# Two layers in one kernel: 64-row products of the state space stage and of the dilated attention, taken in turns between the halves of the array

## The chip, the core and the metric

One core of a Trainium2 chip runs the whole kernel. Its engines are named as in the profile: PE multiplies matrices (PEld is its weight load), DVE and ACT are the two elementwise engines, POOL a third one that does almost nothing here, and SP issues the DMAs. The metric is device time in microseconds (us), the median of several executions. A smaller number is better.

## The reference, cut to what matters

`reference()` is one layer after another on 256 tokens of width 1024, batch 1, all in float32.

```python
x = first_block(...)    # causal attention, gated linear attention, memory attention, a feed-forward of 4096
x = second_block(x, ...)
# second_block:
h = rms_norm_2(x, norm_w)
u_s, z_s, q, k, v, z_a, r_s, r_a = split(h @ w_in)
y_s = s5_branch(u_s, ...)            # per group of 16 channels: h_t = A h_(t-1) + B u_t (64 complex states), Re(C h) + D u
y_s = (y_s * silu(z_s)) @ w_ssm_out
y_a = dilated_attention(rope(norm(q)), rope(norm(k)), v)   # three groups of heads: every, every 4th, every 16th position
y_a = (y_a * silu(z_a)) @ w_attn_out
x = x + (sigmoid(r_s) * y_s + sigmoid(r_a) * y_a) @ w_o
```

The change touches `s5_branch` (64 groups of 16 channels, 64 complex states each) and `dilated_attention` (three groups of 8 heads of 64).

## The kernel before, in words

The layers are written one after the other by the class `Net`, as a list of operations without an order. A planner (`Plan`) then works backward from the end to give each operation a latest time (`latest`), and forward to put them into one order per engine (`order`). It goes by prices in ns that `price` (from L264) gives each instruction, by lags between engines, and by how many buffers there are of each kind (`BUFS`: 8 PSUM banks, 26 large and 11 small SBUF buffers). An engine then runs its instructions strictly in that order, and waits where an operand is late. So a price that changes moves instructions in all engines. Operations written as `nc.any` go to DVE or ACT, as the planner finds. Every instruction is recorded by one helper, hence the line L535 in all rows.

Most of PE's time goes to products with weights (`gemm_feat`, `gemm_tok`). They are split into a high and a low part (tiles `wh`, `wl`) by ACT and DVE, and use the whole array of 128 x 128.

Four functions of the second layer matter here.

- `ssm_quarter` (once for each of four quarters of the groups, `qd`) prepares tables. It has 16 products of 64 rows by 32 columns with 128 moving columns (`p[32 * j:32 * j + 32]`, `kn`). `gh` (0 or 1) picks partitions 0 to 63 or 64 to 127.
- `ssm_scan` (once for each quarter) has 32 products of 64 rows, 64 columns and 64 moving columns into `xp` (`G` with the input `U`); then a chain of DVE work (complex products and two prefix scans, TENSOR_TENSOR_SCAN in the profile) that makes the states `H`; then 48 products of the same size into `y`: for each `gh` and each of eight `g` one of `U` with the table `T`, and two of `H` with `Cx` that are added to it. For `gh` = 0 both operands and the result lie in partitions 0 to 63: the product uses the quarter of the array with rows and columns 0 to 63, called block (0, 0) below. For `gh` = 1 it is block (64, 64). `U` comes back from a bounce through DRAM (`ud`), `T` from another (`kz`).
- `dilated` (four pairs of heads `b`) makes, for each head `i` of a pair and each half `tt` of the tokens, a score tile `p`: one product of all 128 rows, 256 wide (`k2T[0]`), and four of 64 rows, 64 columns, 64 wide. These four have one row half (by the head `i`) and take turns between two column halves (by `c`).
- `block2` starts the parts in turns (`ORDER2`); the planner decides what really stands where.

A float32 product stands in the trace as two matmuls, called halves below: 384 products of 64 x 64 x 64 are 768 rows of the trace. 320 of them belong to `ssm_scan` and 64 to `dilated`.

Of the kernel before, what the change touches and what calls it, by code (L numbers as in the profile page):

```python
# [19 lines left out]
P = 128  # L20
S = 256
# [154 lines left out]
class Plan:  # L176
# [105 lines left out]
    @staticmethod  # L282
    def price(op):

        size = lambda v: int(np.prod(v.shape[1:]))
        if op.name == "dma_start":
            return {SP: 50, ACT: 50, POOL: 1000}[op.eng]
        if op.name == "matmul":
            out, l, r = op.args
            n, cols, half = size(r), size(l), l.shape[0] <= 64  # L290
            if r.buf.dtype == F32R:
                return 13 + n / 2.4
            if cols == 32:
                return 27 if n == 32 else 60
            if cols <= 64 and n <= 64:
                return 110 if half else 142

            if half:
                return 2 * (2 * n / 2.4 + cols / 1.2 - 8)
            return 2 * (max(2 * n / 2.4, cols / 1.2) + 9)  # L300
        if op.name == "transpose":
            return 110
        n = max(size(v) for v in op.outs + op.ins)
        psum = any(v.buf.tag == "ps" for v in op.outs + op.ins)
        if op.eng == ACT:
            c = (51 if psum else 93) + 0.833 * n
            c += 93 * (isinstance(op.kw.get("scale"), View) or isinstance(op.kw.get("bias"), View))
            return c + 93 * ("accum_out" in op.kw)
        if op.eng == POOL:
            return 10 + 0.9 * n if op.name == "memset" else 130 + 2.13 * n  # L310
        ptr = 63 * any(isinstance(a, View) and size(a) == 1 for a in op.args[2:])
        if op.name in ("tensor_copy", "tensor_scalar") and not psum:
            return 68 + 0.52 * n + ptr
        if op.name == "reciprocal":
            return 68 + 6.3 * n
        if op.name == "memset":
            return 10 + 1.05 * n
        return 68 + 1.042 * n + ptr
# [237 lines left out]
class Net:  # L556
# [810 lines left out]
    def ssm_quarter(self, qd):  # L1367
        nc, I = self.nc, self.I
        mag4, pw, f, ph = self.ssm_p
        gs = slice(8 * qd, 8 * qd + 8)  # L1370
        bt, ct = self.bT[:, :, gs], self.cT[:, :, gs]
        over = lambda v, sh: v.unsqueeze(len(v.shape)).to_broadcast(sh)
        sh = [P, 8, 16]
        mk = lambda: self.t2(sh)

        bb = self.t2([P, 2, 8, 16])
        self.cmul((bb[:, 0], bb[:, 1]), (bt[:, 0], bt[:, 1]), (over(f[0][:, gs], sh), over(f[1][:, gs], sh)), mk)
        bbt = self.t2([P, 2, 4, 16, 2])
        for ri in range(2):
            nc.any.copy(bbt[:, ri].rearrange("p j q a -> p j a q"), bb[:, ri].rearrange("p (j a) q -> p j a q", a=2))  # L1380

        cx = self.t4([P, 8, 2, 4, 16])
        nc.any.copy(cx[:, :, 0, 0], ct[:, 0])
        nc.any.copy(cx[:, :, 1, 0], ct[:, 1], -1.0)
        sh3 = [P, 8, 3, 16]
        c0 = tuple(cx[:, :, i, 0:1].to_broadcast(sh3) for i in range(2))
        p3 = tuple(over(pw[:, 1:4, i, gs].rearrange("p t g -> p g t"), sh3) for i in range(2))
        self.cmul((cx[:, :, 0, 1:], cx[:, :, 1, 1:]), c0, p3, lambda: self.t2(sh3), conj=True)

        g0 = self.t4([P, 2, 8, 4, 16])  # L1390
        sh4 = [P, 8, 4, 16]
        b4 = tuple(bb[:, i].unsqueeze(2).to_broadcast(sh4) for i in range(2))
        p4 = tuple(over(pw[:, 5:9, i, gs].rearrange("p t g -> p g t"), sh4) for i in range(2))
        self.cmul((g0[:, 0], g0[:, 1]), b4, p4, lambda: self.t2(sh4))
        gx, g = self.t4([P, 8, 2, 64]), self.t4([P, 8, 2, 64])
        for ri in range(2):
            p = self.mmp([P, 4, P])
            for j in range(4):
                nc.tensor.transpose(p[:, j], g0[:, ri, 2 * j:2 * j + 2].rearrange("p g s q -> p (g s q)"), self.ident)
            nc.any.copy(gx[:, 4 * ri:4 * ri + 4].rearrange("p j g n -> p j (g n)"), p)  # L1400
        for gh in range(2):
            for par in range(2):
                nc.sync.dma_start(out=g[64 * gh:64 * gh + 64, :, par], in_=gx[64 * par:64 * par + 64, :, gh])

        kn = self.t2([P, 2, P])
        for gh in range(2):
            p = self.mmp([P, P])
            hs = slice(64 * gh, 64 * gh + 64)
            for ri in range(2):
                for j in range(4):  # L1410
                    nc.tensor.matmul(p[32 * j:32 * j + 32], bbt[hs, ri, j].rearrange("p q a -> p (q a)"),
                                     cx[hs, 2 * j:2 * j + 2, ri].rearrange("p a t c -> p a (t c)"),
                                     start=ri == 0, stop=ri == 1, skip_group_check=True)
            nc.any.copy(kn[:, gh], p)
            v = kn[:, gh].rearrange("p (a x) -> p a x", a=2)[:, :, 0:16]
            nc.vector.scalar_tensor_tensor(v, self.diag, self.g("d_skip", 4 * gh + qd), v, ALU.mult, ALU.add)
        for par in range(2):
            nc.sync.dma_start(
                out=self.kz[:, par, 4 * qd:4 * qd + 4, :, 48:112].rearrange("g j q x -> (j q) g x"),
                in_=kn[par::2, :, 64 * par:64 * par + 64])  # L1420

        r = self.t4([P, 2, 8, 64])
        nc.vector.memset(r[:, 0, :, 0:1], 1.0)
        nc.vector.memset(r[:, 1, :, 0:1], 0.0)
        k = 1
        for i in range(6):
            shk = [P, 8, k]
            z = tuple(over(ph[:, i, ri, gs], shk) for ri in range(2))
            self.cmul((r[:, 0, :, k:2 * k], r[:, 1, :, k:2 * k]), (r[:, 0, :, 0:k], r[:, 1, :, 0:k]), z, lambda: self.t2(shk))
            k *= 2  # L1430
        self.G.append(g)
        self.Cx.append(cx)
        self.R.append(r)
# [44 lines left out]
    def ssm_scan(self, qd):  # L1478
        nc = self.nc
        mag4 = self.ssm_p[0]  # L1480
        U, G, Cx, R = self.U[qd], self.G[qd], self.Cx[qd], self.R[qd]
        X = self.t4([P, 2, 8, 64])
        xp = [self.aux([P, 8, 64]) for _ in range(2)]
        for ri in range(2):
            for gh in range(2):
                hs = slice(64 * gh, 64 * gh + 64)
                for g in range(8):
                    nc.tensor.matmul(xp[ri][hs, g], G[hs, 4 * ri + g // 2, g % 2], U[hs, g], start=True, stop=True)
            nc.any.copy(X[:, ri], xp[ri])
        mk = lambda: self.t2([P, 8, 64])  # L1490
# [9 lines left out]
        H = self.t4([P, 2, 8, 64])  # L1500
# [1 line left out]
        v = lambda a: a[:, :, 0:63]  # L1502
        self.cmul((H[:, 0, :, 1:], H[:, 1, :, 1:]), (v(st[0]), v(st[1])), (v(R[:, 0]), v(R[:, 1])), lambda: self.t2([P, 8, 63]))
        y = self.aux([P, 8, 64])
        for gh in range(2):
            hs = slice(64 * gh, 64 * gh + 64)
            for g in range(8):
                o = y[hs, g]
                nc.tensor.matmul(o, U[hs, g], self.T[g % 2][hs, 4 * qd + g // 2], start=True, stop=False, skip_group_check=True)
                for ri in range(2):  # L1510
                    nc.tensor.matmul(o, H[hs, ri, g], Cx[hs, g, ri].rearrange("p t c -> p (t c)"), start=False, stop=ri == 1, skip_group_check=True)
        ys = self.t2([P, 4, 8, 16])
        nc.any.copy(ys, y.rearrange("p g (t c) -> p t g c", t=4))
        p = self.aux([P, 4, 2, 64])
# [62 lines left out]
    def dilated(self):  # L1577
# [5 lines left out]
        half = [slice(0, 64), slice(64, P)]  # L1583
        for b in range(4):
            pts = []
            for i, a in enumerate(half):
                prs = []
                for tt in range(2):
                    p = self.aux([P, 384])
                    nc.tensor.matmul(p[:, 0:S], self.q2[0][:, b, tt * P:tt * P + P], self.k2T[0][i][:, b],  # L1590
                                     start=True, stop=False, skip_group_check=True)
                    for j in range(2):
                        for c in range(2):
                            g = 1 + (j ^ c)
                            cs = slice(tt * P + 64 * c, tt * P + 64 * c + 64)
                            nc.tensor.matmul(p[half[c], S + 64 * j:S + 64 * j + 64], self.q2[g][a, b, cs], self.k2T[g][a, b, cs],
                                             start=False, stop=j == 1, skip_group_check=True)
                    pr = self.t2([P, 384])
                    self.softmax_rows(p, pr, [384], self.dmask[:, tt])
                    prs.append(pr)  # L1600
                p0, p1 = self.aux([P, 2, S]), self.aux([P, 2, P])
                for tt in range(2):
                    for kb in range(2):
# [219 lines left out]
```

## Time and profile before

| | |
|---|---|
| median of three runs | 880.23 us (878.02 to 880.57) |
| the profiled execution | 878.85 us, its span 877.1 us |
| PE / DVE / ACT busy | 98% / 73% / 54% of the span |
| granted clock of PE, mean | 0.994 |

The span runs from the first to the last instruction; 1.75 us of the profiled execution lie around it. The first layer ends and the second begins at about 490 us. `ssm_scan` lies between 535 and 646 us, `dilated` between 690 and 725 us, and from there to the end only products with weights are left on PE. Ends of matmuls are modelled, so the pace of PE is best read from the distances of starts.

### The profile page before, as it was taken

The page shows a single profiled execution, that of the slowest core. Times are in us where ns is not written, and L with a number is a line of the kernel's source. Part 1 is how long each engine was busy: PE and PEld are TensorE (multiplying, and loading weights), DVE is VectorE, ACT ScalarE, POOL GpSimd, SP SyncE. Part 2 cuts the span into 40 slices and gives each one's busy share as a digit, 9 for nine tenths or more (in the row PEclk, how much of TensorE's full clock was granted, in tenths as well). Part 3 has the DMA queues.
Part 4 walks back from the last instruction along what each step waited for, and adds up shares of the span by engine and source line. Part 5 has one row for each costly group of instructions (what it writes and reads, how often), then busy time and mean ns, then how long its engine had stood idle before and what let it go on. Part 6 is the DMA issues. An engine that isn't in the chain of part 4 may idle for free.

```text
span 877.1 us, 16677 instructions
## 1 busy us (share of the span) xinstructions
PE 861.0 (98%) x6572; PEld 774.6 (88%) x6572; DVE 636.2 (73%) x1487; ACT 471.6 (54%) x751; POOL 5.4 (1%) x13
## 2 busy tenths in 40 slices
PE   8999998999999999999999998999999999999998
PEld 6988877889999889999999897888889769999996
DVE  6999999994766679954445745898995675653584
ACT  6767756644355466555555542453474663554352
POOL 2000000000000000000000000000000000000000
PEclk9999999999999999999999998999999999999999
DMA  9774432045355565665655579633436503665551
GB/s 322 249 233 145 156 134 98 1 146 191 122 176 184 192 196 192 188 199 189 190 192 191 184 160 248 191 98 114 130 105 190 161 25 105 185 193 183 175 178 64
DMA packets 60750, 144.19 MB, mean 164 GB/s; under 512 B 24560, under 2 KB 25712, under 8 KB 60672
## 3 DMA queue, kind: packets, MB, share of 16 engines
q1 hardware_dynamic: 60672, 143.13, 52.1%
q8 instruction: 51, 0.84, 0.4%
q14 instruction: 27, 0.22, 0.1%
HBM read 138.46 MB, written 2.56 MB: 161 GB/s over the span
## 4 chain that ended last, share of the span: by engine, by line
PE 80%; DVE 12%; DMA 3%; issue 2%; ACT 2%; SPq 1%; DVEq 0%; ACTq 0%
PE ps L535 80%; DVE k L535 7%; DVE wl L535 3%; DVE sm L535 2%; DMA wr<-w_k 1%; ACT k L535 1%; SPq L535 1%; DMA wr<-w_mv 1%; DMA k<-kz 1%; DVE c L535 1%; ACT wh L535 1%; DVEq L1811 0%; ACT c L535 0%; DVEq L535 0%; ACTq L535 0%
## 5 line engine op out<-in xcount | busy, mean ns | idle before, releaser
L535 DVE TENSOR_TENSOR wl<-wr,wh 128x1024 fp32r<-128x1024 f32 (+2 forms) x257 | 301.1, 1195 | 165.6 <-ACT wh L535 163.2
L535 ACT CAST wh<-wr 128x1024 fp32r<-128x1024 f32 (+2 forms) x257 | 257.5, 1028 | 222.6 <-PE ps L535 202.8
L535 PE MATMUL ps<-k,wh 128*128 128x256 f32 x2048 | 371.2, 283 | 0.0
L535 PEld LDWEIGHTS ps<-k,wh 128*128 128x128 f32 x2048 | 320.4, 192 | 1.8 <-ACT c L535 0.3
L535 PE MATMUL ps<-wh,k 128*128 128x512 f32 (+2 forms) x1024 | 314.1, 385 | 2.1 <-ACT wh L535 2.1
L535 PE MATMUL ps<-k,wl 128*128 128x256 f32 x1024 | 290.1, 283 | 0.0
L535 PEld LDWEIGHTS ps<-wh,k 128*128 128x128 f32 x1024 | 190.0, 189 | 38.5 <-ACT wh L535 3.0
L535 PE MATMUL ps<-wl,k 128*128 128x512 f32 (+2 forms) x512 | 197.0, 386 | 1.3 <-DVE wl L535 1.3
L535 PEld LDWEIGHTS ps<-k,wl 128*128 128x128 f32 x1024 | 196.4, 192 | 0.8 <-issue 0.3
L535 PEld LDWEIGHTS ps<-wl,k 128*128 128x128 f32 x512 | 96.6, 189 | 21.1 <-DVE wl L535 3.9
L535 PE MATMUL ps<-k,k 64*64 64x64 f32 (+6 forms) x1224 | 100.4, 256 | 4.4 <-issue 2.3
L535 DVE TENSOR_TENSOR k<-k,k 128x512 f32<-128x512 f32 (+8 forms) x192 | 91.3, 498 | 18.0 <-ACT k L535 17.5
L535 PEld LDWEIGHTS ps<-k,k 64*64 64x64 f32 (+4 forms) x1224 | 78.6, 141 | 21.6 <-issue 12.1
L535 ACT ACTIVATE k<-ps 128x512 f32<-128x512 f32 (+2 forms) x86 | 44.6, 532 | 48.2 <-PE ps L535 48.0
L535 ACT COPY k<-ps 128x512 f32<-128x512 f32 (+7 forms) x97 | 44.2, 497 | 43.9 <-PE ps L535 43.5
L535 ACT ACTIVATE k<-k 128x512 f32<-128x512 f32 (+3 forms) x70 | 46.2, 676 | 32.6 <-DVE k L535 31.8
L535 PE MATMUL ps<-c,k 128*128 128x128 f32 (+1 forms) x344 | 53.4, 285 | 3.5 <-DVE k L535 3.3
L535 PEld LDWEIGHTS ps<-c,k 128*128 128x128 f32 x344 | 41.1, 147 | 11.3 <-DVE k L535 4.8
L535 DVE TENSOR_TENSOR k<-k,c 128x64 f32<-128x64 f32 (+7 forms) x176 | 47.8, 316 | 0.4 <-ACT k L535 0.4
L535 ACT ACTIVATE k<-ps,c 128x256 f32<-128x256 f32 (+3 forms) x78 | 37.8, 544 | 13.6 <-PE ps L535 11.5
L535 DVE SCALAR_TENSOR_TENSOR k<-k,k 128x256 fp32r<-128x256 f32 (+4 forms) x61 | 33.3, 568 | 13.6 <-ACT k L535 13.2
L535 ACT ACTIVATE k<-k,sm 128x384 f32<-128x384 f32 (+2 forms) x32 | 17.0, 531 | 12.7 <-DVE sm L535 12.6
(74 smaller groups left out, 306.2 us busy)
## 6 DMA issues: line engine op xcount, KB each, us to landing
wr<-w_up SPq DMA_DIRECT2D x32, 512.0 KB, 4.0
wr<-w_down SPq DMA_DIRECT2D x32, 512.0 KB, 4.1
wr<-w_gt SPq DMA_DIRECT2D x24, 512.0 KB, 3.8
wr<-w_o SPq DMA_DIRECT2D x16, 512.0 KB, 4.0
wr<-w_k SPq DMA_DIRECT2D x12, 512.0 KB, 4.3
wr<-w_q SPq DMA_DIRECT2D x12, 512.0 KB, 4.4
wr<-w_v SPq DMA_DIRECT2D x12, 512.0 KB, 3.6
wr<-w_qkg SPq DMA_DIRECT2D x8, 512.0 KB, 4.6
```

The source lines that it names most:

```text
L535: getattr(getattr(tc.nc, op.eng), op.name)(*map(live, op.args), **{k: live(v) for k, v in op.kw.items()})
```

## The change

`price` gets 57 in place of 110 ns for a 64-row product with 64 columns, and 30 in place of 60 for those of `ssm_quarter`. In `ssm_quarter` and `ssm_scan` the loop over `gh` becomes the innermost one, so that consecutive products use opposite halves of the rows. In `dilated` the score tiles of both heads of a pair are written together, and the loop over the head is innermost; the softmax follows for both. Neither the products nor their sizes change.

```diff
-                return 27 if n == 32 else 60
+                return 27 if n == 32 else 30
             if cols <= 64 and n <= 64:
-                return 110 if half else 142
+                return 57 if half else 142
...
         for ri in range(2):
-            for gh in range(2):
-                hs = slice(64 * gh, 64 * gh + 64)
-                for g in range(8):
+            for g in range(8):
+                for hs in halves:
                     nc.tensor.matmul(xp[ri][hs, g], G[hs, 4 * ri + g // 2, g % 2], U[hs, g], start=True, stop=True)
...
-        for gh in range(2):
-            hs = slice(64 * gh, 64 * gh + 64)
-            for g in range(8):
-                o = y[hs, g]
-                nc.tensor.matmul(o, U[hs, g], self.T[g % 2][hs, 4 * qd + g // 2], start=True, stop=False, skip_group_check=True)
-                for ri in range(2):
-                    nc.tensor.matmul(o, H[hs, ri, g], Cx[hs, g, ri].rearrange("p t c -> p (t c)"), start=False, stop=ri == 1, skip_group_check=True)
+        for g in range(8):
+            for hs in halves:
+                nc.tensor.matmul(y[hs, g], U[hs, g], self.T[g % 2][hs, 4 * qd + g // 2], start=True, stop=False, skip_group_check=True)
+            for ri in range(2):
+                for hs in halves:
+                    nc.tensor.matmul(y[hs, g], H[hs, ri, g], Cx[hs, g, ri].rearrange("p t c -> p (t c)"), start=False, stop=ri == 1, skip_group_check=True)
...
-            for i, a in enumerate(half):
-                prs = []
-                for tt in range(2):
-                    p = self.aux([P, 384])
-                    nc.tensor.matmul(p[:, 0:S], self.q2[0][:, b, tt * P:tt * P + P], self.k2T[0][i][:, b],
...
+            for tt in range(2):
+                pp = [self.aux([P, 384]) for _ in half]
+                for i in range(2):
+                    nc.tensor.matmul(pp[i][:, 0:S], self.q2[0][:, b, tt * P:tt * P + P], self.k2T[0][i][:, b],
                                      start=True, stop=False, skip_group_check=True)
...
+                for j in range(2):
+                    for c in range(2):
+                        g = 1 + (j ^ c)
+                        cs = slice(tt * P + 64 * c, tt * P + 64 * c + 64)
+                        for i, a in enumerate(half):
+                            nc.tensor.matmul(pp[i][half[c], S + 64 * j:S + 64 * j + 64], self.q2[g][a, b, cs], self.k2T[g][a, b, cs],
...
+                for i in range(2):
                     pr = self.t2([P, 384])
-                    self.softmax_rows(p, pr, [384], self.dmask[:, tt])
-                    prs.append(pr)
+                    self.softmax_rows(pp[i], pr, [384], self.dmask[:, tt])
+                    prs2[i].append(pr)
```

PE, the `y` products of the first quarter. `ps_1437` and `ps_1458` are `y`; rows from `k4_1317` and `k4_1315` (and `k4_1323`, `k4_1319`) are products with `T`, those from `k4_943` products of `H` with `Cx`. Before:

```order
L535 MATMUL ps_1364_6755<-k4_1306_6393,wh_1378_6816 128x256
L535 MATMUL ps_1437_7083<-k4_1317_6514,k4_1329_6578 64x64
L535 MATMUL ps_1437_7083<-k4_943_4369,k4_19_142 64x64 x2
L535 MATMUL ps_1437_7083<-k4_1323_6545,k4_1329_6578 64x64
L535 MATMUL ps_1437_7083<-k4_943_4369,k4_19_142 64x64 x2
L535 MATMUL ps_1437_7083<-k4_1317_6514,k4_1329_6578 64x64
```

And now:

```order
L535 MATMUL ps_1435_7096<-wh_1430_7074,k4_1307_6399 128x512
L535 MATMUL ps_1458_7211<-k4_1315_6498,k4_1320_6539 64x64 x2
L535 MATMUL ps_1458_7211<-k4_943_4369,k4_20_145 64x64 x4
L535 MATMUL ps_1458_7211<-k4_1319_6535,k4_1320_6539 64x64 x2
L535 MATMUL ps_1458_7211<-k4_943_4369,k4_20_145 64x64 x4
L535 MATMUL ps_1458_7211<-k4_1315_6498,k4_1320_6539 64x64 x2
```

Each row holds twice as many, one for each half of the array, in turns. Before, 293 of the 320 products of `ssm_scan` followed directly on one of their own block and 17 on one of the other; now 300 follow on one of the other block and none on one of its own.

PE, the `y` products of the third quarter (`ps_7262` and `ps_7514`; `ps_7365`, `ps_7473` and `ps_7479` are products with the weights of the queries). Before:

```order
L535 MATMUL ps_7262<-k_949_4392,k_1481_7327 64x64
L535 MATMUL ps_7365<-wh_6973,k_1300_6351 128x512
L535 MATMUL ps_7365<-wl_6980,k_1300_6351 128x512
L535 MATMUL ps_7262<-k_949_4392,k_1481_7327 64x64
L535 MATMUL ps_7262<-k_1323_6545,k_1435_7076 64x64
L535 MATMUL ps_7262<-k_949_4392,k_1481_7327 64x64 x2
L535 MATMUL ps_7262<-k_1317_6514,k_1435_7076 64x64
```

And now:

```order
L535 MATMUL ps_7479<-wl_7569,k_1301_6362 128x512
L535 MATMUL ps_7473<-wh_7455,k_1302_6371 128x512
L535 MATMUL ps_7479<-wh_7470,k_1301_6362 128x512
L535 MATMUL ps_7514<-k_950_4393,k_1508_7477 64x64 x2
L535 MATMUL ps_7514<-k_1319_6535,k_1432_7082 64x64 x2
L535 MATMUL ps_7473<-wl_7601,k_1301_6362 128x512
L535 MATMUL ps_7473<-wh_7470,k_1302_6371 128x512
```

The products of `ssm_scan` now stand in 20 separate groups between products with weights; before they stood in 10.

PE, the score tiles of the first pair of heads in `dilated` (before `ps_1685` and `ps_1686`, now `ps_1687` and `ps_1692`). Before:

```order
L535 MATMUL ps_1685_8326<-k4_26_163,k4_1613_7919 128x256
L535 MATMUL ps_1685_8326<-k4_1468_7254,k4_1617_7935 64x64
L535 MATMUL ps_1685_8326<-k4_1589_7809,k4_1628_7985 64x64 x2
L535 MATMUL ps_1685_8326<-k4_1468_7254,k4_1617_7935 64x64
L535 MATMUL ps_1686_8333<-k4_26_163,k4_1613_7919 128x256
L535 MATMUL ps_1686_8333<-k4_1468_7254,k4_1617_7935 64x64
```

And now:

```order
L535 MATMUL ps_1687_8342<-k4_26_163,k4_1572_7770 128x256
L535 MATMUL ps_1687_8342<-k4_1479_7322,k4_1612_7928 64x64
L535 MATMUL ps_1687_8342<-k4_1515_7512,k4_1629_7992 64x64 x2
L535 MATMUL ps_1687_8342<-k4_1479_7322,k4_1612_7928 64x64
L535 MATMUL ps_1692_8354<-k4_29_172,k4_1572_7770 128x256
L535 MATMUL ps_1692_8354<-k4_1479_7322,k4_1612_7928 64x64
```

Here the planner has sorted the products by score tile again. In one of the eight cases (the third pair, one half of the tokens) seven products of two tiles do take turns; in the other seven each tile's four 64-row products stand together, as before.

## Rows read from the trace of the kernel before

**Rows 1.** The page: span, busy time, chain that ended last.
```profile
span 877.1 us, 16677 instructions
...
PE 861.0 (98%) x6572; PEld 774.6 (88%) x6572; DVE 636.2 (73%) x1487; ACT 471.6 (54%) x751; POOL 5.4 (1%) x13
...
PE 80%; DVE 12%; DMA 3%; issue 2%; ACT 2%; SPq 1%; DVEq 0%; ACTq 0%
```

**Rows 2.** Groups of PE's matmuls by shape: shapes, xcount, busy us, mean ns, idle before.
```profile
L535 PE MATMUL ps<-k,k 64*64 64x64 f32 x768 | 45.2, 226 | 3.3 <-issue 2.3 <-DVE k L535 1.0
...
L535 PE MATMUL ps<-k,k 64*32 64x128 f32 x128 | 3.6, 276 | 0.0
```

**Rows 3.** PE in order of time, runs of `ssm_scan`: start us, length us, operation, xcount.
```profile
535.73 4.83 PE L535 MATMUL ps<-k,k 64*64 64x64 f32 x64 [2.33 <-issue]
...
570.95 0.28 PE L535 MATMUL ps<-k,wl 128*128 128x256 f32 x1
571.07 0.28 PE L535 MATMUL ps<-k,wh 128*128 128x256 f32 x1
571.28 3.40 PE L535 MATMUL ps<-k,k 64*64 64x64 f32 x64
574.62 0.39 PE L535 MATMUL ps<-k,wh 128*128 128x256 f32 x1
574.84 0.28 PE L535 MATMUL ps<-k,wl 128*128 128x256 f32 x1
574.96 0.40 PE L535 MATMUL ps<-k,wh 128*128 128x256 f32 x2
...
576.72 8.65 PE L535 MATMUL ps<-k,k 64*64 64x64 f32 x160
...
592.19 5.39 PE L535 MATMUL ps<-k,k 64*64 64x64 f32 x92
...
600.49 2.77 PE L535 MATMUL ps<-k,k 64*64 64x64 f32 x44
...
610.45 5.56 PE L535 MATMUL ps<-k,k 64*64 64x64 f32 x104
...
639.98 5.63 PE L535 MATMUL ps<-k,k 64*64 64x64 f32 x96
```

**Rows 4.** PE in order of time, the products of `ssm_quarter`.
```profile
498.91 0.69 PE L535 MATMUL ps<-k,k 64*32 64x128 f32 x32
...
507.01 0.64 PE L535 MATMUL ps<-k,k 64*32 64x128 f32 x16
```

**Rows 5.** PE in order of time, four score tiles of `dilated`.
```profile
690.70 3.99 PE L535 MATMUL ps<-k,k 128*128 128x256 f32 x40
```

**Rows 6.** Stretches: busy us of each engine, granted clock, DMA.
```profile
535.00:570.00 35.00, 33.97 (x205) 29.23 (x206) 26.83 (x61) 11.64 (x13) 0.00 (x0) 0.90 0.70 204
570.00:650.00 80.00, 78.77 (x813) 69.20 (x812) 74.62 (x170) 39.52 (x63) 0.00 (x0) 1.00 0.40 120
650.00:725.00 75.00, 74.50 (x547) 58.02 (x546) 47.45 (x106) 43.68 (x83) 0.00 (x0) 1.00 0.36 113
```

**Rows 7.** The chain that ended last: start us, us, what.
```profile
574.72 0.59 ACT k L535
...
582.67 8.51 DVE k L535 x20
...
599.57 102.76 PE ps L535 x755
...
706.78 166.73 PE ps L535 x1328
```

**Rows 8.** SP's queue in order of time.
```profile
523.25 5.03 SPq L535 DMA_DIRECT2D k<-kz  x7
...
530.08 0.57 SPq L535 DMA_DIRECT2D k<-ud  x1
```

More of the change, by code (lines that the diff above doesn't have):

```diff
@@ L1405, in ssm_quarter @@
         kn = self.t2([P, 2, P])
-        for gh in range(2):
-            p = self.mmp([P, P])
-            hs = slice(64 * gh, 64 * gh + 64)
-            for ri in range(2):
-                for j in range(4):
-                    nc.tensor.matmul(p[32 * j:32 * j + 32], bbt[hs, ri, j].rearrange("p q a -> p (q a)"),
+        kp = [self.mmp([P, P]) for _ in range(2)]
+        for ri in range(2):
+            for j in range(4):
+                for gh in range(2):
+                    hs = slice(64 * gh, 64 * gh + 64)
+                    nc.tensor.matmul(kp[gh][32 * j:32 * j + 32], bbt[hs, ri, j].rearrange("p q a -> p (q a)"),
                                      cx[hs, 2 * j:2 * j + 2, ri].rearrange("p a t c -> p a (t c)"),
                                      start=ri == 0, stop=ri == 1, skip_group_check=True)
-            nc.any.copy(kn[:, gh], p)
+        for gh in range(2):
+            nc.any.copy(kn[:, gh], kp[gh])
             v = kn[:, gh].rearrange("p (a x) -> p a x", a=2)[:, :, 0:16]
@@ L1483, in ssm_scan @@
         xp = [self.aux([P, 8, 64]) for _ in range(2)]
+        halves = [slice(64 * gh, 64 * gh + 64) for gh in range(2)]
         for ri in range(2):
-            for gh in range(2):
-                hs = slice(64 * gh, 64 * gh + 64)
-                for g in range(8):
+            for g in range(8):
+                for hs in halves:
                     nc.tensor.matmul(xp[ri][hs, g], G[hs, 4 * ri + g // 2, g % 2], U[hs, g], start=True, stop=True)
@@ L1504, in ssm_scan @@
         y = self.aux([P, 8, 64])
-        for gh in range(2):
-            hs = slice(64 * gh, 64 * gh + 64)
-            for g in range(8):
-                o = y[hs, g]
-                nc.tensor.matmul(o, U[hs, g], self.T[g % 2][hs, 4 * qd + g // 2], start=True, stop=False, skip_group_check=True)
-                for ri in range(2):
-                    nc.tensor.matmul(o, H[hs, ri, g], Cx[hs, g, ri].rearrange("p t c -> p (t c)"), start=False, stop=ri == 1, skip_group_check=True)
+        for g in range(8):
+            for hs in halves:
+                nc.tensor.matmul(y[hs, g], U[hs, g], self.T[g % 2][hs, 4 * qd + g // 2], start=True, stop=False, skip_group_check=True)
+            for ri in range(2):
+                for hs in halves:
+                    nc.tensor.matmul(y[hs, g], H[hs, ri, g], Cx[hs, g, ri].rearrange("p t c -> p (t c)"), start=False, stop=ri == 1, skip_group_check=True)
         ys = self.t2([P, 4, 8, 16])
@@ L1585, in dilated @@
             pts = []
-            for i, a in enumerate(half):
-                prs = []
-                for tt in range(2):
-                    p = self.aux([P, 384])
-                    nc.tensor.matmul(p[:, 0:S], self.q2[0][:, b, tt * P:tt * P + P], self.k2T[0][i][:, b],
-                                     start=True, stop=False, skip_group_check=True)
[L1592 to L1596, printed above, removed]
+            prs2 = [], []
+            for tt in range(2):
+                pp = [self.aux([P, 384]) for _ in half]
+                for i in range(2):
+                    nc.tensor.matmul(pp[i][:, 0:S], self.q2[0][:, b, tt * P:tt * P + P], self.k2T[0][i][:, b],
+                                     start=True, stop=False, skip_group_check=True)
+                for j in range(2):
[4 more added lines that the diff above has]
+                            nc.tensor.matmul(pp[i][half[c], S + 64 * j:S + 64 * j + 64], self.q2[g][a, b, cs], self.k2T[g][a, b, cs],
                                              start=False, stop=j == 1, skip_group_check=True)
+                for i in range(2):
                     pr = self.t2([P, 384])
-                    self.softmax_rows(p, pr, [384], self.dmask[:, tt])
-                    prs.append(pr)
+                    self.softmax_rows(pp[i], pr, [384], self.dmask[:, tt])
+                    prs2[i].append(pr)
+            for prs in prs2:
                 p0, p1 = self.aux([P, 2, S]), self.aux([P, 2, P])
```

## The prediction

> **What bounds the kernel now.** I read the page first: PE is busy 98% of the span, and the chain that ended last is PE for 80% and DVE for 12% of it [rows 1]. So time taken from PE is time taken from the kernel, except where the chain lies on another engine. The stretches show where that is: from 570 to 650 us, where most of the state space products lie, DVE is busy 74.62 of 80 us beside PE's 78.77; before that, from 535 to 570, DVE has 8.2 us free, and from 650 to 725 it has 27.6 [rows 6]. The chain in order of time agrees: it runs over DVE (with one ACT step) from 574.72 to 599.57, 25 us, then over PE for the next 103 us, and over PE for 167 us at the end [rows 7]. There, from 706.78, PE runs products with weights that the change leaves in their order; whatever is gained before should arrive at the end in full.
>
> Then I read PE's runs of 64 x 64 products. The busy time of a group (45.2 us for 768 halves, mean 226 ns each [rows 2]) is no pace, since a half's shown length covers its way through the array; the pace is length less about 0.22 us, divided by the steps. The run of 44 halves, all in one block, gives (2.77 - 0.22) / 43 = 0.059 us a half; the run of 64, which changes blocks three times, (3.40 - 0.22) / 63 = 0.050 [rows 3]. If all 64 had gone one by one at 0.059, the run would be 0.5 us longer: already now some halves on either side of a change of block run side by side.
>
> **The change part by part.**
>
> *Pace of the state space products.* The seven large runs hold 624 of the 640 halves; the other 16 stand in four small runs. Their lengths are 3.40, 3.40 (in place of 4.83, which fell into a stretch of half clock: rows 6 have 0.90 as the mean granted clock of 535 to 570), 8.65, 5.39, 2.77, 5.56 and 5.63 us, together 34.80 [rows 3]. Of each, 0.16 us is the end of the last half beyond its step (0.22 less 0.06), which leaves 33.7 us, or 0.054 us a half, 34.5 us for 640.
>
> What does a half cost when blocks (0, 0) and (64, 64) take turns? No run does this throughout, but two groups come near. In `ssm_quarter`, 32 halves with both row halves in one run took 0.69 us, and 16 of one row half alone 0.64 [rows 4]: 16 more cost 0.05 us, so the second row half runs beside the first nearly for nothing. In `dilated`, where products take turns between two column halves, four score tiles, each two halves of a 256-wide product and eight of 64 x 64, took 3.99 us [rows 5], 1.0 us each; eight 64 x 64 halves alone would be 0.47 at 0.059, and a 256-wide half moves four times as many columns (0.059 x 4 = 0.23 each), so one by one a tile would be 0.93 before the changes of shape, some 0.3 (below): above the 1.0 seen. So two blocks side by side it is, 0.059 us for a pair, 0.0293 a half: 640 x 0.0293 = 18.7 us, and the pace gives 34.5 - 18.7 = 15.8 us. The other bound is that nothing runs side by side, 0.059 x 640 = 37.8, a loss of 3.3 us. I take 15.8, since rows 4 show just such a second row half.
>
> The Trainium skill has a rule here that cuts the gain. "TensorE: Matmul & The Clock Gate", Part 3, under "The mechanism", says that matmuls start and end strictly in program order. By that rule a product's second half (one block, 0.059 behind its first) would hold back the first half of the other block, and a pair of products would take 2 x 0.059 and two short steps between blocks, some 0.13 in place of 0.117; the sum would be smaller by about 2 us. Rows 4 speak against so strict a rule: 32 halves in the time of 16 leave no room for one block to wait for another.
>
> *More visits.* To go from products with weights to 64 x 64 products and back costs time. Around the run at 571.28: the last start before lies 0.21 us ahead in place of 0.12; the next two starts behind lie 0.15 us behind the last half's start (574.47) in place of 0.06, and 0.22 in place of 0.12; and I add 0.05 for the run's own first step. That is 0.09 + 0.09 + 0.10 + 0.05 = 0.33 us a visit [rows 3]. The order has 20 visits in place of 10: 3.3 us lost. It may be less where PE would have waited anyway; at most the ten are free (0). The Trainium skill names the reason: "TensorEngine Tiling (Array Packing)", under "Key Properties", has it that a change of tiling mode drains the array, while a change of block in one mode does not. The trace agrees, with the 0.33 us.
>
> *The tables' products* (`ssm_quarter`). Both row halves run side by side already wherever the planner put them into one run [rows 4]; the whole group is 3.6 us [rows 2]. I count 0; only the runs of one row half could gain, 0.6 us at most.
>
> *Dilated.* The order shows that the planner undoes the turns between the heads in seven of eight cases; the two column halves ran side by side before. One case gains some 0.2 us. Two score tiles are begun early and hold two PSUM banks through some 30 us of products with weights, which have six left; each such product group uses two. I count -0.2 us.
>
> *What is late next.* PE is 15.8 - 3.3 = 12.5 us shorter between 535 and 646 us. From 570 to 650 lie 576 halves, so 576 x 0.0247 = 14.2, less some 3 us of visits: 11.2 us shorter. DVE could give 5.4 us there (80 - 74.62 [rows 6]). If the DVE work stayed in this stretch, 5.8 us would come back as waits of PE for DVE. It need not stay: DVE has 8.2 us free ahead and 27.6 behind, and the new order puts products with the queries' weights, and so their splits on DVE, between the first scans. Bounds 0 and 5.8; I take the middle, 3 us, since the rows say nothing of which part moves.
>
> *The start of the first scan.* PE already waits 2.33 us at 535.73 [rows 3] for the input's bounce through DRAM. Its load stood on SP behind seven loads of the table `T`, 5.03 us or 0.72 each [rows 8]; now nine stand there. That is up to 1.4 us more, or nothing where the load waits for its store anyway; I take 0.7. Half clock followed on this wait; that it stays as it is, is the likeliest.
>
> **The sum.** 878.85 (1.75 of it around the span) - 12.5 - 0.2 + 3 + 0.7 = 869.85 us; I predict 870. The profiled execution lies 1.4 us below the median of the runs, 880.23, and inside their range.
>
> **The rivals.**
>
> *DVE takes over.* All DVE work stays between 570 and 650 us, and the 5.8 us come back: 878.85 - 12.5 - 0.2 + 5.8 + 0.7 = 872.7. For it: DVE at 93% there. Against it: free time on both sides.
>
> *The chain of scans.* While the chain lies on DVE (574.72 to 599.57 [rows 7]) PE's products only fill its time, and nothing that is saved there counts. Then only the runs from 600.49 on gain: 44 + 104 + 8 + 96 = 252 halves x 0.0247 = 6.2 us, less the 3.3 of the visits, which makes 876: close to no change. Against it: PE waits almost nowhere in these 25 us, so it has other products to bring forward.
>
> *Half clock goes away.* The first run, 4.83 us where its like took 3.40 [rows 3], and some 2 us behind it would be saved: 870 - 3.4, about 866.5. It needs PE not to stop at 535 us, or not long enough; the order gives no reason for that.
>
> *Slower: the blocks do not run side by side in steady turns.* Side by side as now, at a change after eight products, might need a queue of one block's work ahead of the other; single turns might not give it. Then the pace falls to 0.059 a half, 3.3 us are lost as above, and 3.3 for visits: 885.5. It decides from where a pair of halves costs more than 0.108 - 0.010 = 0.098 us: above that, 640 halves and ten visits cost more than the 34.5 us of now. Rows 4 speak against it; there, though, four blocks of a row half stand in a row.
>
> **Chances and range.** This forecast 0.57 (866 to 873 as its own range), DVE takes over 0.19, half clock away 0.08, chain of scans or other waits to within 0.3% 0.09, blocks not side by side or waits that eat more than the gain 0.07. About 0.3%, 2.6 us, is what a measurement of this kernel can tell from no change. The first three are faster: 0.84; 876 and what lies around 878 to 882 is the same in part, 0.09; slower 0.07. The range is 863 to 876.5: down to half clock away with free visits, up to the chain of scans.
>
> **What would show it.** In the profile after, a run of 64 halves of `ssm_scan` alone would take some 2.1 us in place of 3.40 (32 pairs x 0.059, and 0.22); starts should come in pairs. All visits together should hold about 19 us of steps. If the runs shrink and the span does not, PE's waits between 570 and 650 us should name DVE, and DVE should be busy above 95% there. The score tiles of `dilated` should take 1.0 us each as before. The prediction is wrong if the runs keep 0.05 us a half, if PE waits for DVE over 6 us in this stretch, or if the wait before the first scan grows beyond 4 us.

## The result and the profile after

The changed kernel takes 865.12 us (median of four runs, 864.48 to 865.86); the kernel before, run beside it, 879.44 us (878.02 to 880.57). The ratio is 0.983, with a 95% interval of 0.981 to 0.985: faster, by 14.3 us or 1.7%. The forecast was 870 (863 to 876.5). So the direction and the range held, and 5 us of the gain were not foreseen.

The profiled execution took 864.48 us. Its page, in the lines that answer to [rows 1]:

```profile
span 862.7 us, 16680 instructions
...
PE 845.5 (98%) x6572; PEld 757.2 (88%) x6572; DVE 630.5 (73%) x1484; ACT 471.6 (55%) x754; POOL 5.4 (1%) x13
...
PE 84%; DVE 9%; DMA 2%; ACT 1%; issue 1%; SPq 1%; DVEq 0%; ACTq 0%
```

The span is 14.4 us shorter and PE is as full as before. The groups of PE's matmuls by shape, which answer to [rows 2]:

```profile
L535 PE MATMUL ps<-k,k 64*64 64x64 f32 x768 | 29.6, 223 | 1.6 <-DMA k<-ud 0.6 <-DVE k L535 0.5 <-ACT k L535 0.4
...
L535 PE MATMUL ps<-k,k 64*32 64x128 f32 x128 | 2.6, 274 | 0.0
```

The mean of one is still 223 ns, but the group's busy time, in which overlapping halves count once, fell from 45.2 to 29.6 us. PE in order of time shows the same in single runs (start us, length us, xcount, idle time ahead in brackets), as [rows 3] did:

```profile
532.27 0.33 PE L535 MATMUL ps<-k,k 64*64 64x64 f32 x4 [0.64 <-DMA k<-ud]
...
533.92 1.96 PE L535 MATMUL ps<-k,k 64*64 64x64 f32 x60
...
568.35 0.28 PE L535 MATMUL ps<-k,wh 128*128 128x256 f32 x1
568.56 2.08 PE L535 MATMUL ps<-k,k 64*64 64x64 f32 x64
570.57 0.39 PE L535 MATMUL ps<-k,wh 128*128 128x256 f32 x1
570.79 0.28 PE L535 MATMUL ps<-k,wl 128*128 128x256 f32 x1
...
577.45 1.15 PE L535 MATMUL ps<-k,k 64*64 64x64 f32 x32
...
585.96 3.02 PE L535 MATMUL ps<-k,k 64*64 64x64 f32 x96
```

A run of 64 takes 2.08 us in place of 3.40 (forecast: 2.1), so a half costs (2.08 - 0.22) / 63 = 0.0295 us. The starts in this run come 6 ns and 100 ns, and then 7, 52, 6, 52, ... ns behind each other: in pairs. The first wait fell from 2.33 to 0.64 us, and the run behind it is no longer stretched.

The products of `ssm_quarter`, as in [rows 4]:

```profile
498.45 1.40 PE L535 MATMUL ps<-k,k 64*32 64x128 f32 x64
...
502.33 1.18 PE L535 MATMUL ps<-k,k 64*32 64x128 f32 x64
```

The stretches of [rows 6] (busy us of PE, PEld, DVE, ACT and POOL, granted clock, DMA):

```profile
535.00:570.00 35.00, 32.84 (x239) 27.89 (x236) 32.01 (x70) 15.45 (x19) 0.00 (x0) 1.00 0.72 222
570.00:650.00 80.00, 78.83 (x831) 63.91 (x828) 72.19 (x164) 44.94 (x70) 0.00 (x0) 1.00 0.38 125
650.00:725.00 75.00, 74.33 (x593) 60.31 (x593) 48.15 (x111) 41.59 (x83) 0.00 (x0) 1.00 0.35 114
```

DVE works 5 us more than before between 535 and 570 us and 2.4 us less between 570 and 650. These are fixed times, and PE is 2.7 us ahead of the old run at the second scan and 11.7 us at the end of the last, so each stretch holds a later piece of the program; the part on the prediction compares the same pieces. The clock is 1.00 in the first stretch, where it was 0.90. PE's waits from 520 to 862 us (us in total, how often, longest) and pieces of the chain that ended last, which answers to [rows 7]:

```profile
PE ps L535 <- DVE wl L535: 2.2, 2, 1.9
PE ps L535 <- DVE k L535: 1.1, 3, 0.6
PE ps L535 <- DMA k<-ud: 0.6, 1, 0.6
PE ps L535 <- ACT k L535: 0.6, 2, 0.4
```

```profile
552.13 27.15 PE ps L535 x217
579.30 1.06 ACT wh L535
...
591.20 6.21 DVE k L535 x16
...
606.19 22.27 PE ps L535 x180
...
629.80 58.76 PE ps L535 x442
```

The chain still runs over DVE for some 27 us (579.30 to 606.19, where the runs of 32, 96 and 50 halves lie), but PE waits hardly at all in them. From the first product of `ssm_quarter` to the first product with weights behind `dilated`, I added up the distances of PE's starts by kind:

| us | before | after |
|---|---|---|
| 640 halves of `ssm_scan` | 37.3 | 22.0 |
| 128 halves of `ssm_quarter` | 3.2 | 2.4 |
| `dilated`, all products | 23.9 | 22.7 |
| products with weights | 137.6 | 138.9 |
| transposes (152 and 160; eight stood ahead of this stretch) | 19.0 | 20.2 |
| PE idle | 4.7 | 5.7 |
| sum | 225.8 | 211.9 |
| of it at half clock (granted 0.5) | 6.8 | 0 |

From there to PE's end both take 148.77 us: whatever was gained before arrived at the end, as the prediction had it.

### The profile page after: what moved, and what is told of

It reads as the page before. It is cut to its first block, busy times and chain, and to the rows that moved or that the text cites. A ratio compares the mean times of both kernels' runs of the same rounds, so it can differ in the third digit from the quotient of the medians.

```text
span 862.7 us, 16680 instructions
## 1 busy us (share of the span) xinstructions
PE 845.5 (98%) x6572; PEld 757.2 (88%) x6572; DVE 630.5 (73%) x1484; ACT 471.6 (55%) x754; POOL 5.4 (1%) x13
## 4 chain that ended last, share of the span: by engine, by line
PE 84%; DVE 9%; DMA 2%; ACT 1%; issue 1%; SPq 1%; DVEq 0%; ACTq 0%
PE ps L535 84%; DVE k L535 6%; DVE wl L535 2%; DVE sm L535 1%; SPq L535 1%; ACT k L535 1%; DMA wr<-w_mv 1%; DMA wr<-w_k 1%; ACT wh L535 0%; DMA k<-k 0%; DVE c L535 0%; DVEq L1815 0%; ACTq L535 0%; DVEq L535 0%
## 5 line engine op out<-in xcount | busy, mean ns | idle before, releaser
L535 PE MATMUL ps<-k,k 64*64 64x64 f32 (+6 forms) x1224 | 83.5, 253 | 2.6 <-ACT k L535 1.4
L535 PEld LDWEIGHTS ps<-k,k 64*64 64x64 f32 (+4 forms) x1224 | 62.4, 139 | 21.3 <-issue 12.3
```

Source lines behind the costliest of these rows:

```text
L535: getattr(getattr(tc.nc, op.eng), op.name)(*map(live, op.args), **{k: live(v) for k, v in op.kw.items()})
```

## Experiments

The kernel before, run beside them, had medians of 879.46 us (with the first four) and 879.83 us (with the last four). "Theory" and "rival" are those of each expectation.

### The new prices alone

```diff
 kernel before
-                return 27 if n == 32 else 60
+                return 27 if n == 32 else 30
...
-                return 110 if half else 142
+                return 57 if half else 142
```

> Before with the two new prices alone; no product takes turns. Theory (the gain is the pace of the state space products, the new order costs a little): the halves keep 0.054 us, the products stand in 20 groups in place of 10, so 879.4 + 3.3 = 882 us, between 879 and 884. Rival (the new order made most of it, by the shorter first wait and the half clock that went away): 5 us or more faster, 874 us or less, with no half clock at 537 us.

Measured: 879.85 us, ratio 1.001 (0.9995 to 1.002). The planner's new order, with 20 groups of `ssm_scan` and the old turns, is worth nothing. PE in order of time shows the old pace:

```profile
568.22 3.40 PE L535 MATMUL ps<-k,k 64*64 64x64 f32 x64
```

By the sums of starts the order costs 5.2 us: its scan halves take 37.5 us, 1.6 more than the 35.9 that the kernel before would need without its half clock, and products with weights and transposes take 3.6 more in the same way (the eight moved transposes, 1.0 us, left out). It gives back 3.4 us, since its first wait is 0.49 us and no half clock follows in this stretch. The time lies at the lower end of the theory's range, but not by its sum alone: the order costs 5.2 us in place of 3.3, and what the rival named, no half clock, did come and gave 3.4 back.

### The turns of `ssm_scan` alone

The kernel before with the loops of `ssm_scan` as in the change; prices, `ssm_quarter` and `dilated` as before.

> Before with turns in the scans alone, at the old prices: 11 groups, 307 of 320 products follow one of the other block. Theory: 640 halves at 0.0293 us in place of 0.054 give 15.8, one more visit takes 0.3, so 864 us, with 2 to 3 more if half clock stays; between 862 and 868. Rival (PE runs ahead of the old plan, waits for DVE and loses half of it again): 871 us or more, with PE's waits for DVE over 6 us between 570 and 650.

Measured: 876.27 us, ratio 0.996 (0.994 to 0.997): 3.2 us of the 14.3. The rival's time was right. The halves take 22.4 us in all (22.0 in the changed kernel), but PE idles 16.5 us in place of 4.7. Between 570 and 650 us it waits 5.2 us for DVE, where the rival had over 6, and 2.1 for a load of `U` and 3.7 for ACT besides. Its waits from 520 to 880 us:

```profile
PE ps L535 <- DVE k L535: 5.7, 6, 2.4
PE ps L535 <- ACT k L535: 3.7, 1, 3.7
PE ps L535 <- issue: 2.4, 1, 2.4
PE ps L535 <- DVE wl L535: 2.3, 2, 2.1
PE ps L535 <- DMA k<-ud: 2.1, 1, 2.1
```

And the stretch of 570 to 650 us, with two of the waits in order of time:

```profile
570.00:650.00 80.00, 69.02 (x814) 58.70 (x810) 74.70 (x173) 40.12 (x66) 0.00 (x0) 0.96 0.37 120
```

```profile
596.78 0.33 PE L535 MATMUL ps<-k,k 64*64 64x64 f32 x4 [2.35 <-DVE k L535]
...
643.14 1.42 PE L535 MATMUL ps<-c,k 128*128 128x128 f32 x9 [3.72 <-ACT k L535]
```

DVE does as much work in this stretch as before (74.62 us [rows 6]), and PE, faster now, runs out of other products. With the old prices the planner takes PE to be busy for 110 ns a product; that it brings too little forward for that reason is argued, not shown. Half clock came three times, 3.4 us each; the third followed the wait of 3.72 us. Prices alone are worth 0, the turns of the scans alone 3.2, and the whole change 14.3 (11.9 without `dilated`, by the next run): prices and turns need each other.

### The change without `dilated`

`dilated` as before, all else as in the change.

> The changed kernel with the dilated attention as it was. Theory (in three of eight cases the score products of both heads did meet, and PE's steps in the dilated attention fell by 1.4 us): 866.5 us, 1 to 2 us slower than the changed kernel. Rival (it brings nothing, PE waits there anyway): 865 us, the same.

Measured: 867.61 us, ratio 0.986 (0.985 to 0.988), 2.5 above the changed kernel. In its profile the products of `dilated` take 23.5 us in place of 22.7, so 0.8 of it is `dilated` itself, where the theory had 1.4. The rest fits the clock: the timed runs have a mean granted clock of 0.9942 in place of 0.9968, which is about 1.6 us by the reckoning below. This profile too has 3.4 us of half clock in the stretch, behind a first wait of 1.8 us, and the changed kernel's has none, though the order is the same in both up to the second scan.

### Longer turns

```diff
 kernel after
-            for g in range(8):
-                for hs in halves:
-                    nc.tensor.matmul(xp[ri][hs, g], ...)
+            for g0 in (0, 4):
+                for hs in halves:
+                    for g in range(g0, g0 + 4):
+                        nc.tensor.matmul(xp[ri][hs, g], ...)
...
             for hs in halves:
                 nc.tensor.matmul(y[hs, g], U[hs, g], ...)
-            for ri in range(2):
-                for hs in halves:
+                for ri in range(2):
                     nc.tensor.matmul(y[hs, g], H[hs, ri, g], ...)
```

> The changed kernel with longer turns in the scans: four products (8 halves) of a block in a row for xp, three (6 halves) for y. Theory (PE takes in work of the other block some 3 halves ahead, as the changes of block before showed: three pairs at each): y keeps 0.0293 us a half, xp gets 0.0366 (5 steps for 8 halves), 256 x 0.0073 = 1.9 us more: 867 us. Rival 1 (it looks far enough ahead for any of these turns): 865 us and all halves at 0.0293. Rival 2 (only strict turns run side by side): all halves at 0.05, 640 x 0.02 = 13 us more: 878 us.

Measured: 867.19 us, ratio 0.986 (0.985 to 0.988), 2.1 above the changed kernel; the theory had 867. That the times agree is in part luck: the scan halves take 25.5 us in place of 22.0, 3.5 more and not 1.9, but PE comes to the first scan later here and does not wait at all, where the changed kernel waits 0.64 us. Both rivals fail by the pace. A run of 64 halves in turns of eight:

```profile
567.75 2.69 PE L535 MATMUL ps<-k,k 64*64 64x64 f32 x64
```

That is (2.69 - 0.22) / 63 = 0.039 us a half; turns of six halves (`y`) come to 0.031, turns of two to 0.0295, turns of sixteen (before) to 0.050. Sixteen halves in turns of eight take 16 x 0.039 = 0.63 us, which is 10.7 steps of 0.0585: some 2.7 halves run beside others at each change of block. Whatever reaches further ahead than about three halves waits.

### Twice the work on PE

In the changed kernel each `xp` product is issued twice in a row (256 halves more, the same values). The order is the same, but a turn of `xp` is now four halves long; its runs keep 0.0297 us a half.

> The changed kernel, in its own order, with each of the 128 products of xp issued twice (the second writes the same values again). 256 halves more, at 0.0293 us: 7.5 us of PE. Theory (with the new order PE sets the end in the scans too): 865.1 + 7.5 = 872.6, between 870.5 and 874. Rival (DVE has already taken over between 570 and 650, PE has slack there): under 869.

Measured: 871.49 us, ratio 0.990 (0.989 to 0.992), 6.4 above the changed kernel, for 256 x 0.0293 = 7.5 us of halves. Most of it arrives at the end, as the theory had it: PE sets the end in this stretch, and its time is not filler beside the chain of scans.

### Score products of both heads kept together

A new field `group` gives all products of one pair of heads and one half of the tokens the same rank in the planner, so that they keep the order in which `dilated` writes them.

```diff
 kernel after
...
+        for op in ops:
+            if op.group:
+                most[op.group] = max(most.get(op.group, -1e18), op.prio)
+        for op in ops:
+            if op.group:
+                op.prio = most[op.group]
...
                 pp = [self.aux([P, 384]) for _ in half]
+                self.plan.group = "score", b, tt
...
```

> The changed kernel, with the ten score products of both heads of a pair held at one rank in the planner, so that they stand together: row halves now take turns in all eight cases (56 changes of row half in place of 9). Theory (four blocks side by side, eight halves in the time of four): some 0.4 us less in each of the five cases that are new, 863 us. Rival (the softmax on DVE and ACT decides here, or both heads' tiles come too late): 865 us or more.

Measured: 862.51 us, ratio 0.981 (0.979 to 0.983), 2.6 us below the changed kernel, where 863 was expected. Two score tiles of a pair in this kernel:

```profile
681.22 1.62 PE L542 MATMUL ps<-k,k 128*128 128x256 f32 x20
```

Less the last half's end, 1.40 us for two tiles, 0.70 each; by the same reckoning it was (3.99 - 0.22) / 4 = 0.94 before [rows 5]. Sixteen 64 x 64 halves start in fours, 7 ns apart, 0.016 us a half on average: all four blocks of the array work side by side. The pace shows the gain better than the time does: the two intervals overlap, and of the 3.6 us between the two spans 1.4 lie in the stretch of the table above and 2.2 ahead of it, where both kernels have the same order.

### Products into `y` kept together, and both groups

The same field for the products into `y`, with `H` ahead of `T`, so that a quarter's 48 products stand in one piece (13 groups of `ssm_scan` in place of 20); then with that of `dilated`.

```diff
 kernel after
+        self.plan.group = "y", qd
         for g in range(8):
-            for hs in halves:
-                nc.tensor.matmul(y[hs, g], U[hs, g], ...)
-            for ri in range(2):
+            for ri in (1, 0):
                 for hs in halves:
                     nc.tensor.matmul(y[hs, g], H[hs, ri, g], ...)
+            for hs in halves:
+                nc.tensor.matmul(y[hs, g], U[hs, g], ...)
```

> The changed kernel, with the 48 products of y held at one rank and the products of H first, so that all wait for H: 13 groups in place of 20. Theory (a visit costs 0.33 us): 7 x 0.33 = 2.3 us less, 862.8 us. Rival (the early products with T filled PE's waits for H): 866 us or more, with longer waits for DVE.

Measured: 865.59 us, ratio 0.984 (0.982 to 0.986): no gain on the changed kernel.

> Both of these together. Theory: the gains add up, 861 us. Rival: the planner's new order costs as much as it gains, 865 us or more.

Measured: 863.25 us, ratio 0.981 (0.979 to 0.983): no gain on 862.51. Both theories failed. In the first of the two the rival's time, 866 or more, was the nearer: PE waits longer for DVE and ACT, 5.8 us in place of 3.9, and has 3.4 us of half clock in this stretch besides. Its waits:

```profile
PE ps L542 <- DVE wl L542: 3.1, 3, 2.1
PE ps L542 <- DVE sm L542: 1.2, 1, 1.2
PE ps L542 <- DVE k L542: 0.9, 2, 0.6
PE ps L542 <- ACT k L542: 0.6, 2, 0.4
```

Of the two kernels with the group of `dilated`, neither has half clock in this stretch, so their starts can be set side by side: with seven groups fewer the scan halves take 1.3 us less and the products with weights and transposes 0.7 less, 0.30 us a visit. PE's idle time is 1.1 us longer (7.5 in place of 6.4). What is left, under 1 us, is less than the medians of four and five runs can tell. That the longer waits are why nothing shows is argued, not shown.

## Why the prediction was right, and where its size was off

The profiled executions are 14.4 us apart; the sum had 9.0.

*Pace: right.* 15.8 us forecast; 640 x (0.054 - 0.0295) = 15.7 measured. The rule of the Trainium skill that was weighed there ("TensorE: Matmul & The Clock Gate", Part 3, "The mechanism": starts and ends strictly in program order) does not agree with the trace. By it a product's second half would lie between the first halves of the two blocks, the first step of a run would be 59 ns and the mean about 33; the first step is 6 ns and the mean 29.6. The kernel before shows it too: where it changes blocks after sixteen halves, three pairs start 4 to 6 ns apart, and strict order would allow one. The rival "slower" falls with this, but its worry, a queue that sees only so far, is real: it is what the longer turns show.

*Visits: 3.3 forecast, 0.30 x 10 = 3.0 by the last two kernels.* The planner's order as a whole costs 5.2 us, though, with the new prices alone; in the changed kernel it comes to the same by the same sums (scans 22.0 less 18.9 at full pace, where before it was 1.4 above; products with weights and transposes 3.4). The 2 us beyond the visits lie in products with weights and transposes; I can't assign them further.

*Waits for DVE: the mis-sized term.* It had +3, from the bounds 0 and 5.8, for PE's waits between 570 and 650 us. The lower bound came: PE idles 1.2 us there in both kernels. The reason given against the rival "DVE takes over" holds: DVE's work did not stay. Read between the same products (the second scan's first and the last of all scans; first before, then after):

```profile
571.28:645.45 74.17, 72.94 (x773) 64.10 (x772) 68.98 (x152) 34.19 (x51) 0.00 (x0) 1.00 0.41 122
...
568.56:633.70 65.14, 63.97 (x783) 51.61 (x782) 58.47 (x139) 33.70 (x51) 0.00 (x0) 1.00 0.36 114
```

PE's 9.0 us less go with 10.5 us less of DVE; between the first scan and the second DVE has 31.1 us of work in place of 27.3, and the rest went behind the scans. That it would not have moved so far by itself is shown by the turns alone: there DVE has 64.5 of 68.0 us between the same products and PE waits 7.3, 5.2 of it for DVE. That rival holds for the same products under the old prices. The changed kernel's waits for DVE and ACT still are 3.9 us in place of 2.0, because a wait came in the stretch that was counted as free, for a split of weights behind DVE's work on the first scan:

```profile
545.34 0.39 PE L535 MATMUL ps<-k,wl 128*128 128x256 f32 x1 [1.89 <-DVE wl L535]
```

*The first scan's wait: the step that failed.* It forecast +0.7 us, since nine loads of `T` stand ahead of the load of `U` in place of seven. It fell by 1.7. The store that this load reads stood on SP before at:

```profile
522.77 0.39 SPq L535 DMA_DIRECT2D ud<-k  x1
```

SP's queue after, as in [rows 8]:

```profile
519.14 0.58 SPq L535 DMA_DIRECT2D ud<-k  x1
519.90 4.65 SPq L535 DMA_DIRECT2D k<-kz  x7
...
525.57 0.91 SPq L535 DMA_DIRECT2D k<-kz  x2
526.54 0.44 SPq L535 DMA_DIRECT2D k<-ud  x1
```

I counted what lies ahead of the load and not when the queue comes to it. The store into `ud` stands at 519.14 us in place of 522.77; the nine loads begin 3.4 us earlier, and the load of `U` leaves 3.5 us earlier, by which PE's first scan could start 3.5 us earlier. The size of this wait isn't the order's alone: three kernels with the changed kernel's order up to here show 1.6, 1.8 and 2.5 us, against its own 0.64. All four lie below the forecast's 3.0, but that it fell by as much as 1.7 here is luck. Nor was it worth 1.7: what PE gained at the first scan it waited for at 545.34. The first wait and the next long one come to 0.64 + 1.89 = 2.5 us, before to 2.33 + 0.30 = 2.6. In the kernel without `dilated` (1.84 us, and 3.4 us of half clock behind it) the wait for the split is gone, and the second scan starts 70.9 us behind the first product of `ssm_quarter`, in the changed kernel 70.1.

*Half clock: the rival that came true beside the forecast.* It had 866.5 at a chance of 0.08, "the order gives no reason". The order gave one, the same early load, though no certainty. In the profile before, 6.8 us at half clock cost 3.4 us; after, there is none in this stretch. It isn't the turns that do it: the prices alone lose it too, the turns alone have 10.2 us of it. Nor is it fixed by the order, as the doubled kernel and the one without `dilated` show (3.4 us long each, at the first scan); that the changed kernel's profile has none is in part luck. The timed runs bear it out: their mean granted clock has a median of 0.992 in 28 runs of the kernel before, 0.9965 in the four after. Between runs of one kernel, 0.002 less clock went with 1.3 us more time, so by this estimate about 2.9 of the 14.3 us come from the clock.

*Dilated and the tables: -0.2 and 0 forecast, -1.2 and -0.8 measured.* I read one case of eight as gaining. In three, products of the two heads adjoin at the tiles' boundary, and there four blocks worked side by side at 0.017 to 0.019 us a half. The tables' runs gained what was named as their most, 0.6, and a little more.

Against the sum of 9.0: half clock 3.4, the first wait 2.4, waits for DVE 1.1, `dilated` 1.0 and the tables 0.8 more were gained, 8.7; the order cost 1.9 more (5.2 in place of 3.3), and 1.4 went into short gaps on PE (0.8) and what changed its place at the stretch's ends. These are sums by kind, and not what each is worth alone: the first wait and the wait for DVE belong together, +3.7 forecast and +0.2 measured. The forecast's mechanism held. Its error is, in the main, the 3 us for DVE between 570 and 650 us that did not come and the half clock that went; the record on SP was read by position and not by time, and little hung on it in the end.

## What to carry over

When a bound engine gets faster at one kind of work, its planner has to be told: the turns gave 3.2 us under the old prices and 11.9 under the new (both without those of `dilated`; the second with those of the tables, 0.8), and the new prices without the turns nothing. Products of a quarter of the array should change blocks with every product, through all the blocks there are (58.5 ns a half in one, 29.5 in two, 16 in four), and a scheduler that sorts them again needs a reason not to. To say whether a load comes later, compare the times at which its store and the queue get there, not the number of loads ahead; and look for the wait behind it, which may take back what is gained.

## What the runs showed of the hardware

- Halves of other blocks start ahead of a waiting half of the same block, but only some three halves ahead: 0.0295 us a half in turns of two halves, 0.0297 of four, 0.031 of six, 0.039 of eight, 0.050 of sixteen.
- Half clock on PE, 3.4 or 6.8 us long in this stretch, came with waits of PE of 1.8 to 3.7 us (1.84, 2.06 twice, 2.09, 2.33, 2.5 and 3.72; it began 0.3 us before the end of the 2.5, and 0.1 to 1.4 us behind the others), but not with each: 1.89 us in the changed kernel, 2.04 in that with both groups, 2.06 in that of the longer turns, and 2.36 and 2.35 in that of the turns alone passed without it. A stretch with it (0.66 is the mean of 3.4 us at half clock and the rest at full), behind the wait of 2.06 us at 544.89 in the kernel with the products into `y` together:

```profile
545.00:550.00 5.00, 5.00 (x19) 4.13 (x20) 5.00 (x11) 0.00 (x0) 0.00 (x0) 0.66 0.75 240
```
